# The way from the output projection to the up projection: second norm's gains moved into the weights, halves of the products interleaved with turns

## The chip, the cores and the metric

One Trainium2 chip, one core of it. TensorE (PE) multiplies, VectorE (DVE), ScalarE (ACT) and GpSimd (POOL) work on the results, and SyncE (SP) issues every DMA from one queue, in order. Each engine works through its own list of instructions in order and waits at the first one whose inputs or buffers are not ready. The metric is the time of one execution on the device, in microseconds (us): the median of three runs.

## The reference

One layer of an encoder: 1024 positions, 1024 channels, all in float32. What matters here is the step from the mixing sub-layer to the channel sub-layer.

```
y = concat(rmsnorm(ya, out_norm_a), rmsnorm(yb, out_norm_b)) @ w_o
x = x + rmsnorm(y, norm_mix_post)
h = rmsnorm(x, norm_ffn_pre)          # h = x / rms(x) * gain, gain has one value per channel
u = dwconv(h @ w_up, conv_w, conv_b)  # w_up: 1024 x 5632, width-3 convolution along the sequence
g, v = u[..., :2816], u[..., 2816:]
y = (gelu(g) * v) @ w_down
x = x + rmsnorm(y, norm_ffn_post)
```

## The kernel before

**Products.** Every float32 matrix is split into a high part that the multiplier takes exactly and a low part (ACT copies the high part, DVE or POOL subtracts it from the source), and a product is three matmuls: high by high, high by low, low by high. An instruction multiplies a 128x128 weight by 128x512 columns.

**The mixing sub-layer** ends with the output projection `o`, eight tiles of 128 positions (`t` = 0 to 7). Each tile takes 24 matmuls in two halves of 512 channels (`o_steps`, L1097); a half's accumulator is evacuated by DVE (L1107). Tiles 0 and 1 run under the last attention heads (events written at times of a plan); tiles 2 to 7 are written out by hand at L1301 to L1340. The rows that tile `t` needs are copied and split by `o_rows` (L1088): half of them are read from DRAM (`yd2`, L1090), the other half are in SBUF (`B["y"]`) once the last heads are normalised (`finish_steps`, L275).

**Two norms** follow for each tile (`o_norms`, L1111): ACT squares and sums the row, the root is taken, DVE or POOL multiplies by the gain of the first norm (L1117: on POOL for tiles 2 to 5), DVE scales and adds the residual (L1118), the sum is stored (L1119), ACT squares again, and DVE multiplies by root and by the second gain, `gffn` (L1123). That gain is read twice from DRAM as a 128x1024 broadcast.

**The up projection** works on 22 column tiles `f`. For each it has a tile `g` and a tile `v` of weights (loaded by `up_raw`, 512 KB each) and makes seven products (`up_product`, L1244), numbered 1 to 7, in place of the eight half-sized products of a 2x2 block scheme: weights are combined first (`up_prep`, L1225: DVE forms the sum `S`, ACT and POOL split it), the activations are combined too (`late_sums`, L1280), and the results are added afterwards (L1264 to L1274). A product is 12 matmuls. Each combination of the activations (5, 6, 7, 3, 4; 1 and 2 need none) is turned by TensorE: `late_turn` (L1290) does four 128x128 transposes into one of two PSUM banks `tr`, ACT copies the high part out, DVE the low part. The sums need both halves of the sequence, so tiles 4 to 7 decide.

**Order around the change.** The order of the calls is the priority; the framework then fixes each engine's list when the kernel is built, by its own estimate of when inputs are ready. `tc.issue_after(x)` holds a block's instructions behind instruction x on x's engine. After the hand-written o tiles, products (f, n) = (0,1), (0,2), (1,1), (1,2) run, each followed by the sums and four turns of one tile (L1352), then the turns for combination 4, then the remaining ten products of f = 0 and 1 in pairs (L1411), then f = 2 to 21, seven products each. Weights are prepared five products ahead (`AHEAD`). When the last product of an f is done, `conv_gate(f)` (L1372) does the convolution, the gelu and the gate with ACT and DVE.

**Buffers.** A new tile takes the memory of tiles freed before and waits for their last users. PSUM has eight banks of 128x512: two for `om` (o halves and small sums), two for `tr`, and four for `u`, the accumulators of even f, at this point. Copies `c1` of product 1 lie in a pool (`h2q`) that covers the memory of the o stage (`po`).

Of the kernel before, what the change touches and what calls it, by code (L numbers as in the profile page):

```python
# [37 lines left out]
def layer_kernel(  # L38
# [122 lines left out]
    gcols = cp.t([P, 16], "gcols")  # L161
# [256 lines left out]
    def small_columns():  # L418

        gr = pa.t([P, 512], "ph", bufs=PH)[:16, :P]  # L420
# [9 lines left out]
        nc.tensor.transpose(pt[:, 384:397], gr[:13, :], ident[:13, :13])  # L430
        nc.vector.tensor_copy(cvt.rearrange("p a b -> p (a b)"), pt[:, : 8 * NFF])
        nc.vector.tensor_copy(gcols[:, :13], pt[:, 384:397])
# [655 lines left out]
    def o_rows(q, yt, ys):  # L1088
        cs = slice(256 * q, 256 * q + 256)
        nc.sync.dma_start(yt, yd2[:, :, cs].rearrange("k p t -> p k t"))  # L1090
# [20 lines left out]
    def o_norms(t, junk, gpost, gffn, rsqrt=rsqrt_newton):  # L1111
# [11 lines left out]
        nc.vector.scalar_tensor_tensor(y, x2, rr, gffn, op0=ALU.mult, op1=ALU.mult)  # L1123
# [7 lines left out]

    def early_tiles():
        O["gpost"] = w4("wh")
        nc.sync.dma_start(O["gpost"], g_mix_post.partition_broadcast(P))
        O["gffn"] = w4("wh")
        nc.sync.dma_start(O["gffn"], g_ffn_pre.partition_broadcast(P))
# [9 lines left out]
    def early_norms(t):  # L1146
        o_norms(t, pa.t([P, S], "tmp", bufs=2), O["gpost"], O["gffn"])

    EARLY, EARLY_N = 2, 2
    NORM_V, NORM_P = [0, 1, 6, 7], [2, 3, 4, 5]  # L1150
# [38 lines left out]
    def late_rows(q):  # L1189
        ys = two_ys() if q == 2 else [xr.t([P, 2, 4, P], "x4", F32R), O["p"].t([P, 2, 4, P], "ys", F32R)]  # L1190
        o_rows(q, quarter_tile(po, QB), ys)
# [7 lines left out]
    def late_o(t):  # L1199
        for f in o_steps(t, om_bank):  # L1200
            f()

    def late_norms(t):
        o_norms(t, junk.pop() if junk else po.t([P, D], "jk"), gpost, gffn, rsqrt_cols)
# [3 lines left out]
    RAW, PREP, SUM = {}, {}, {}  # L1208

    def up_raw(f):  # L1210
        RAW[f] = []
        for w in range(2):
# [3 lines left out]
            RAW[f].append(wf)  # L1216

    count = []

    def w_tile():  # L1220

        count.append(0)
        return (pf if len(count) <= 4 or len(count) % 2 else pf2).t([P, 2, 4, P], "w", F32R, bufs=4)

    def up_prep(f, n):  # L1225
        if f not in RAW:
            up_raw(f)
# [4 lines left out]
        if n in terms:  # L1232
            src = SUM[f, n] = pf2.t([P, 4, P], "S", bufs=4)
# [8 lines left out]
    UP, MOV, CP = {}, {}, {}  # L1242

    def up_product(f, n):  # L1244
        if n == 1:
            if f % 2 == 0:
                UP[f] = [pu0.t([P, 2, 512], "u", bufs=2) for _ in range(2)]
# [10 lines left out]
        for k in range(4):  # L1258
            first, last = n in (1, 5, 2) and k == 0, k == 3
            mm(bank, w[:, 0, k], m[:, 0, k], start=first, stop=False, skip_group_check=True)  # L1260
            mm(bank, w[:, 0, k], m[:, 1, k], start=False, stop=False, skip_group_check=True)  # L1261
            mm(bank, w[:, 1, k], m[:, 0, k], start=False, stop=last, skip_group_check=True)  # L1262
        if n in (1, 5, 6):
            CP[f, n] = CP.pop("first", None) or (cpp if n == 1 else ap_).t([P, 512], f"c{n}", bufs=2)  # L1264
# [8 lines left out]
        if n == 3:  # L1273
            nc.vector.tensor_tensor(bank, bank, CP[f, 6], op=ALU.add)  # L1274

# [4 lines left out]
    def late_sums(t):  # L1280
# [4 lines left out]
        nc.vector.tensor_tensor(l[:, K0], h[:, K0], l[:, K0], **sub)  # L1285
        nc.gpsimd.tensor_tensor(h[:, K0], h[:, K1], h[:, K0], **sub)
        nc.vector.tensor_tensor(t2, h[:, K1], l[:, K0], **sub)
        nc.gpsimd.tensor_tensor(l[:, K1], l[:, K1], t2, **sub)
# [12 lines left out]
    gffn = bcast_row(po, g_ffn_pre, "gffn")  # L1301
# [3 lines left out]
    gpost = bcast_row(po, g_mix_post, "gpost")  # L1305
    fin = finish_steps(3, B, [], (2, 3), lambda: quarter_tile(po, QB), om_bank)
# [10 lines left out]
    fin[7]()  # L1317
    early_transpose(1)
    late_rows(2)
    late_norms(2)  # L1320
    group_rsqrt(1, slice(4, 8), rsqrt_cols)
    late_rows(3)
# [5 lines left out]
    late_o(4)  # L1328
    early_transpose(2)
    late_norms(4)  # L1330
    late_o(5)
    early_transpose(3)
    late_norms(5)
    up_raw(1)
    late_o(6)
    late_norms(6)
    late_o(7)
    for n in (1, 2):
        up_prep(1, n)
    late_norms(7)  # L1340
    po.free()
    O["p"].free()
    pwo.free()
    pu1 = {"v": Pool("pu1v", space=PSUM)}
    h2q = Pool("h2T1")
    MOV.update({1: B0[:, :, 0:4], 2: B0[:, :, 4:8]})
    MOV[4] = h2q.t([P, 2, 4, 512], "T4", F32R)
    cpp = h2q
    CP["first"] = h2q.t([P, 512], "c1", bufs=2)
    for n in (5, 6, 7, 3):  # L1350
        MOV[n] = h2q.t([P, 2, 4, 512], f"T{n}", F32R)
    for t, (f, n) in zip(range(4, 8), ((0, 1), (0, 2), (1, 1), (1, 2))):  # L1352
        up_product(f, n)
        late_sums(t)
        for n in (5, 6, 7, 3):
            late_turn(t, n)
    for t in range(4, 8):
        late_turn(t, 4)
# [52 lines left out]
    seq = [(f, n) for n in (5, 6, 7, 3, 4) for f in range(2)] + [(f, n) for f in range(2, NFF) for n in ORDER]  # L1411
# [238 lines left out]
```

## Time and profile before

| | |
|---|---|
| median of 3 runs | 1500.83 us (1500.44 to 1502.06) |
| profiled execution | 1505.44 us, its span 1503.4 us |
| PE busy | 1416.5 us, 94% of the span, 6481 matmuls |
| DVE, ACT, POOL busy | 972.3, 704.9, 533.2 us |
| mean granted clock of TensorE | 0.970 |

The span is the time from the first to the last instruction. A granted clock of 1.00 is TensorE at 2.4 GHz, 0.50 is 1.2 GHz. Attention ends at about 778 us of the span, the o tiles and norms lie between 756 and 846 us, and from 905 us on the up projection runs its regular pattern to about 1300 us.

### The profile page before, as it was taken

Reading aid. Unit: us, or ns where it says so; the run is one execution under the profiler, and the core shown is the slowest. Engines: PE = TensorE matmul, PEld = TensorE weight load, DVE = VectorE, ACT = ScalarE, POOL = GpSimd, SP = SyncE. Lnnn points to the kernel's source line nnn. Section 1 sums busy time; section 2 is a strip of 40 time slices with the busy share of each in tenths; the row PEclk is TensorE's granted clock in tenths of the full one; section 3 lists DMA queues with packets and bytes.
Section 4 is the critical chain, followed back from the end, with each engine's and each line's share of the span. In section 5 each row is a group of like instructions: output and inputs, shape, how many; then the busy total and the mean of one; then the engine's idle time right before and its main releaser. Section 6 shows DMA issues by size and latency. Waiting matters only on the chain.

```text
span 1503.4 us, 18725 instructions
## 1 busy us (share of the span) xinstructions
PE 1416.5 (94%) x6481; PEld 1120.9 (75%) x6481; DVE 972.3 (65%) x1637; ACT 704.9 (47%) x1274; POOL 533.2 (35%) x443
## 2 busy tenths in 40 slices
PE   7999999997899999889998689999999999999998
PEld 6788887876676676556666567888888888788886
DVE  6465453438976766532487768766677765884687
ACT  5244343325455556534645354444444444554444
POOL 3133222216444544322425355555555553000110
PEclk9999999997999999989999899999999999999999
DMA  5522343555433212521116123333333321964435
GB/s 188 118 72 67 76 101 87 169 134 187 99 70 104 63 36 69 145 75 29 57 56 205 48 70 112 106 106 105 105 105 106 106 91 58 336 219 144 126 98 196
DMA packets 135903, 167.06 MB, mean 111 GB/s; under 512 B 17443, under 2 KB 93616, under 8 KB 134144
## 3 DMA queue, kind: packets, MB, share of 16 engines
q1 hardware_dynamic: 135808, 165.87, 37.2%
q8 instruction: 51, 0.84, 0.2%
q14 instruction: 44, 0.36, 0.1%
HBM read 106.12 MB, written 39.43 MB: 97 GB/s over the span
## 4 chain that ended last, share of the span: by engine, by line
PE 52%; DVE 5%; POOL 4%; ACT 3%; issue 3%; DMA 2%; SPq 0%; DVEq 0%; POOLq 0%; ACTq 0%
PE u_pu L1260 4%; PE u_pu L1262 4%; PE u_pu L1261 4%; PE v_pu1v L1260 3%; PE v_pu1v L1262 3%; PE v_pu1v L1261 3%; PE X_acc L1501 2%; PE X_acc L1502 2%; PE X_acc L1500 2%; PE Y_acc L1501 2%; PE Y_acc L1500 2%; PE Y_acc L1502 2%; PE g_pu1g L1260 2%; PE g_pu1g L1262 2%; PE g_pu1g L1261 2%
## 5 line engine op out<-in xcount | busy, mean ns | idle before, releaser
L348 POOL TENSOR_TENSOR pl_pA<-sx_pA,ph_pA 128x512 fp32r<-128x512 f32 (+1 forms) x125 | 162.8, 1307 | 266.3 <-ACT sx_pA L92 122.7
L1240 POOL TENSOR_TENSOR w_pF<-S_pF,w_pF 128x512 fp32r<-128x512 f32 x88 | 129.4, 1472 | 106.3 <-ACT w_pF L92 77.0
L1240 POOL TENSOR_TENSOR w_pF<-wf_pF,w_pF 128x512 fp32r<-128x512 f32 x66 | 88.9, 1349 | 96.7 <-ACT w_pF L92 96.6
L95 PE MATMUL proj_psx<-hT_hT,wh_pA 128*128 128x512 f32 (+2 forms) x304 | 120.6, 397 | 0.0
L96 PE MATMUL proj_psx<-hT_hT,wh_pA 128*128 128x512 f32 (+2 forms) x304 | 119.0, 391 | 0.1
L97 PE MATMUL proj_psx<-hT_hT,wl_pA 128*128 128x512 f32 (+2 forms) x304 | 118.9, 391 | 0.0
L945 DVE TENSOR_REDUCE m_pA<-mx_psy 128x1 f32<-128x512 f32 x126 | 83.9, 685 | 38.9 <-PE mx_psy L944 38.3
L92 ACT ACTIVATE w_pF<-ar_pD 128x512 fp32r<-128x512 f32 x77 | 48.5, 630 | 99.6 <-PE Y_acc L1502 44.0
L92 ACT ACTIVATE w_pF<-S_pF 128x512 fp32r<-128x512 f32 x88 | 55.3, 628 | 80.2 <-PE u_pu L1262 41.2
L92 ACT ACTIVATE sx_pA<-s_ps 128x512 f32<-128x512 f32 x128 | 75.0, 597 | 27.9 <-PE s_ps L970 13.2
L1260 PE MATMUL u_pu<-T_h2T,w_pF 128*128 128x512 f32 x220 | 85.7, 390 | 1.5 <-ACT c_h2T L92 1.5
L1262 PE MATMUL u_pu<-T_h2T,w_pF 128*128 128x512 f32 x220 | 85.7, 390 | 0.6 <-POOL w_pF L1240 0.6
L1261 PE MATMUL u_pu<-T_h2T,w_pF 128*128 128x512 f32 x220 | 85.8, 390 | 0.0
L1462 DVE TENSOR_TENSOR w_pF<-ar_pD,w_pF 128x512 fp32r<-128x512 f32 x77 | 55.5, 721 | 46.3 <-ACT w_pF L92 46.3
L337 DVE TENSOR_TENSOR sx_pA<-s_ps,tab_pA 128x256 f32<-128x256 f32 (+1 forms) x128 | 48.3, 410 | 53.4 <-PE s_ps L607 34.1
L537 DVE CUSTOM_DVE_ANT_0 mx_psx<-mx_psx,tab_pA 128x256 f32<-128x256 f32 (+1 forms) x112 | 47.1, 420 | 48.9 <-PE mx_psx L534 45.6
L229 POOL TENSOR_TENSOR wl_pA<-wf_pA,wh_pA 128x256 fp32r<-128x256 f32 x48 | 36.9, 794 | 115.0 <-ACT wh_pA L92 102.3
L348 DVE TENSOR_TENSOR pl_pA<-sx_pA,ph_pA 128x512 fp32r<-128x512 f32 (+1 forms) x67 | 48.7, 730 | 35.9 <-ACT sx_pA L92 34.2
L1501 PE MATMUL X_acc<-w_pF,w_pF 128*128 128x512 f32 x176 | 68.9, 391 | 2.4 <-DVE w_pF L1464 2.4
L92 ACT ACTIVATE ph_pA<-s_ps 128x512 fp32r<-128x512 f32 x85 | 50.4, 596 | 38.6 <-PE s_ps L970 38.2
L1500 PE MATMUL X_acc<-w_pF,w_pF 128*128 128x512 f32 x176 | 68.5, 389 | 0.0
L1502 PE MATMUL X_acc<-w_pF,w_pF 128*128 128x512 f32 x176 | 68.5, 389 | 0.0
(451 smaller groups left out, 4143.8 us busy)
## 6 DMA issues: line engine op xcount, KB each, us to landing
wf_pF<-in_w_up SPq DMA_DIRECT2D x44, 512.0 KB
ar_pD<-aD_dr SPq DMA_DIRECT2D x77, 256.0 KB
head_pA<-x_xr SPq DMA_DIRECT2D x22, 512.0 KB
aD_dr<-vt_aT SPq DMA_DIRECT2D x44, 256.0 KB
B_pD<-in_w_down SPq DMA_DIRECT2D x44, 256.0 KB
aD_dr<-gt_aT SPq DMA_DIRECT2D x33, 256.0 KB
wf_pA<-in_w_in SPq DMA_DIRECT2D x16, 512.0 KB
head_pA<-x_xr SPq DMA_DIRECT2D x24, 256.0 KB
```

What stands on the lines that cost most here:

```text
L92: nc.scalar.activation(o, i, func, **kw)
L95: i = mm(ps, ah, bh, start=first, stop=False)
L96: mm(ps, ah, bl, start=False, stop=False)
L97: mm(ps, al, bh, start=False, stop=last)
L348: e.tensor_tensor(pl[:, cs], pf[:, cs], f32(ph[:, cs]), op=ALU.subtract)
L1240: nc.gpsimd.tensor_tensor(w[:, 1], src, f32(w[:, 0]), op=ALU.subtract)
L1260: mm(bank, w[:, 0, k], m[:, 0, k], start=first, stop=False, skip_group_check=True)
L1261: mm(bank, w[:, 0, k], m[:, 1, k], start=False, stop=False, skip_group_check=True)
L1262: mm(bank, w[:, 1, k], m[:, 0, k], start=False, stop=last, skip_group_check=True)
L1500: mm(bank, wa[:, 0, ts], wb[:, 0], start=first, stop=False, skip_group_check=True)
L1501: mm(bank, wa[:, 0, ts], wb[:, 1], start=False, stop=False, skip_group_check=True)
L1502: mm(bank, wa[:, 1, ts], wb[:, 0], start=False, stop=last, skip_group_check=True)
```

## The change

The second norm's gain is no longer multiplied into the rows. It is read once as columns (`gcols` 13 to 20, in `small_columns`), and ACT multiplies it into the raw weights, one 128x128 block at a time and in place (`up_scale`): 16 blocks for each f, all of f = 0 and of f = 1 at once, and for later f four blocks at each of four of the preparations of the f before. The load of the next f is written one f earlier. In `o_norms` the last step becomes an ACT scaling by the root, and all first-gain products go to DVE. Both broadcasts of `gffn` are gone.

The rows of the last two quarters are loaded into tiles of their own early on (`late_rows_load`). The o tiles of even t use two `u` banks in place of `om`. The first four products follow the last o tile at once, ahead of the norms of tiles 6 and 7. The copies `c1` move to the pool `h2p`, the first `S`, `c5` and `c6` tiles to memory that is free earlier. The turns of combination 5 come behind product (1,2); each of the turns for 6, 7, 3 and 4 is cut in two pairs, one ahead of and one inside the product of f = 0 before it. The POOL half of the sums is a function of its own behind them (`late_sums2`). The five products of f = 0 run first, `conv_gate(0)` follows them, then the five of f = 1.

```diff
@@ small_columns
-        for r0, src in ((0, g_q), (3, g_kv), (5, g_a), (9, g_b)):
+        for r0, src in ((0, g_q), (3, g_kv), (5, g_a), (9, g_b), (13, g_ffn_pre)):
...
@@ o_norms
-        nc.vector.scalar_tensor_tensor(y, x2, rr, gffn, op0=ALU.mult, op1=ALU.mult)
+        act(y, x2, scale=rr)
...
+    def late_rows_load(q):
+        cs = slice(256 * q, 256 * q + 256)
+        YQ[q] = (O["p"] if q == 2 else po).t([P, 512], "yq").rearrange("p (k t) -> p k t", k=2)
+        nc.sync.dma_start(YQ[q], yd2[:, :, cs].rearrange("k p t -> p k t"))
...
-    NORM_V, NORM_P = [0, 1, 6, 7], [2, 3, 4, 5]
+    NORM_V = range(NT)
...
     def late_o(t):
-        for f in o_steps(t, om_bank):
+        bank = om_bank
+        if t % 2 == 0:
+            u = pu0.t([P, 2, 512], "u", bufs=2)
+            halves = [u[:, 0, :], u[:, 1, :]]
+            bank = lambda: halves.pop(0)
+        for f in o_steps(t, bank):
             f()
...
+    def up_scale(n):
+        for wf, k in SCALE[:n]:
+            act(wf[:, k], wf[:, k], scale=gcols[:, 13 + k : 14 + k])
+        del SCALE[:n]
...
     def up_prep(f, n):
-        if f not in RAW:
-            up_raw(f)
+        if 0 < f < NFF - 1 and f + 1 not in RAW and (f, n) != (1, 1) and (f, n) != (1, 2):
+            up_raw(f + 1)
+        elif n not in (1, 5):
+            up_scale(4)
...
         for k in range(4):
+            if k == 2 and mid:
+                mid()
...
-            CP[f, n] = CP.pop("first", None) or (cpp if n == 1 else ap_).t([P, 512], f"c{n}", bufs=2)
+            CP[f, n] = C0.pop() if f == 0 and n > 1 else (h2p if n == 1 else ap_).t([P, 512], f"c{n}", bufs=2)
...
+    late_rows(2)
+    group_rsqrt(1, slice(4, 8), rsqrt_cols)
+    late_norms(2)
+    late_rows(3)
     early_transpose(1)
...
+    up_scale(16)
     for n in (1, 2):
         up_prep(0, n)
...
+    for f in range(2):
+        for n in (1, 2):
+            early = up_product(f, n)
+    late_norms(6)
     late_norms(7)
...
-    for t, (f, n) in zip(range(4, 8), ((0, 1), (0, 2), (1, 1), (1, 2))):
-        up_product(f, n)
-        late_sums(t)
-        for n in (5, 6, 7, 3):
+    for t in range(4, 8):
+        summed = late_sums(t)
+    def turn_two(n, t):
+        if n:
             late_turn(t, n)
+            late_turn(t + 1, n)
+    with tc.issue_after(early.ins):
+        turn_two(5, 4)
+        turn_two(5, 6)
     for t in range(4, 8):
-        late_turn(t, 4)
+        late_sums2(t)
+    for n, after in zip((5, 6, 7, 3, 4), (6, 7, 3, 4, None)):
+        with tc.issue_after(summed.ins):
+            up_prep(0, n)
+        turn_two(after, 4)
+        up_product(0, n, lambda: turn_two(after, 6))
...
-    seq = [(f, n) for n in (5, 6, 7, 3, 4) for f in range(2)] + [(f, n) for f in range(2, NFF) for n in ORDER]
+    conv_gate(0)
+    seq = [(1, n) for n in (5, 6, 7, 3, 4)] + [(f, n) for f in range(2, NFF) for n in ORDER]
```

## Rows read from the trace of the kernel before

**Rows 1.** Windows: us, then busy us (x instructions) per engine, PE clock, DMA

```profile
785.00:845.00 60.00, 46.76 (x215) 37.34 (x213) 50.25 (x70) 29.97 (x64) 31.23 (x18) 0.93 0.48 158
838.00:854.00 16.00, 7.41 (x27) 5.42 (x26) 12.17 (x13) 5.17 (x10) 7.11 (x5) 0.68 0.08 33
...
785.20:905.40 120.20, 95.64 (x430) 74.59 (x429) 91.46 (x120) 61.05 (x112) 57.22 (x37) 0.91 0.32 101
...
1000.00:1190.40 190.40, 190.40 (x841) 157.66 (x841) 132.97 (x141) 90.75 (x131) 99.16 (x70) 1.00 0.32 104
```

**Rows 2.** Timeline of PE: start, duration, instruction, [idle before it, releaser]

```profile
798.25 0.50 PE L95 MATMUL om_pwo<-w_wo,qr_qr 128*128 128x512 f32 x1 [2.99 <-ACT qr_qr L92]
...
800.69 0.80 PE L97 MATMUL om_pwo<-w_wo,qr_qr 128*128 128x512 f32 x1 [1.48 <-DVE qr_qr L1059]
801.29 0.63 PE L95 MATMUL om_pwo<-w_wo,qr_qr 128*128 128x512 f32 x1
801.71 0.63 PE L96 MATMUL om_pwo<-w_wo,qr_qr 128*128 128x512 f32 x1
...
822.53 0.47 PE L95 MATMUL om_pwo<-w_wo,ys_wo 128*128 128x512 f32 x1 [1.39 <-DVE x_xr L1107]
...
844.99 0.80 PE L1260 MATMUL v_pu1v<-h2T_h2T,w_pF 128*128 128x512 f32 x1 [6.36 <-ACT c_h2T L92]
...
880.19 0.50 PE L1260 MATMUL v_pu1v<-T_h2T,w_pF 128*128 128x512 f32 x1 [2.12 <-DVE g_pu1g L1270]
...
905.37 0.50 PE L1260 MATMUL u_pu<-T_h2T,w_pF 128*128 128x512 f32 x1 [1.50 <-ACT c_h2T L92]
```

**Rows 3.** Timeline of SP: loads of the second gain and of the rows

```profile
780.71 0.37 SPq L206 DMA_DIRECT2D gffn_pO<-in_norm_ffn_pre  x1
...
794.05 1.65 SPq L1090 DMA_DIRECT2D tmp_pO<-yd_dr  x2
```

**Rows 4.** Timeline of ACT between 790 and 845 us

```profile
797.78 0.72 ACT L92 ACTIVATE qr_qr<-tmp_pO 128x256 fp32r<-128x256 f32 x2 [1.49 <-DMA tmp_pO<-yd_dr]
...
842.90 0.58 ACT L92 ACTIVATE c_h2T<-u_pu 128x512 f32<-128x512 f32 x1
```

**Rows 5.** Groups on ACT: count | busy us, mean ns | idle before, releaser

```profile
L92 ACT ACTIVATE w_wo<-wf_pA,gcols_const 128x1024 fp32r<-128x1024 f32 x8 | 9.2, 1149 | 14.7 <-DMA wf_pA<-in_w_o 14.7
...
L92 ACT ACTIVATE ckv_lat<-x_xr 128x1024 fp32r<-128x1024 f32 x2 | 2.0, 1041 | 0.0
...
L92 ACT ACTIVATE wf_pA<-wf_pA 128x128 f32<-128x128 f32 x2 | 0.5, 303 | 1.7 <-DMA wf_pA<-in_w_in 1.7
```

**Rows 6.** Groups on DVE and POOL, the same columns

```profile
L1235 DVE TENSOR_TENSOR S_pF<-S_pF,wf_pF 128x512 f32<-128x512 f32 x22 | 27.3, 1239 | 10.2 <-POOL w_pF L1240 10.0
...
L1123 DVE SCALAR_TENSOR_TENSOR x_xr<-xt_pO,r_const,gffn_pO 128x1024 f32<-128x1024 f32 x4 | 8.1, 2030 | 0.1
...
L1117 DVE TENSOR_TENSOR PA_woA<-PA_woA,wh_pA 128x1024 f32<-128x1024 f32 x2 | 2.4, 1217 | 0.0
...
L1117 POOL TENSOR_TENSOR x_xr<-x_xr,gpost_pO 128x1024 f32<-128x1024 f32 x2 | 6.1, 3046 | 6.8 <-ACT jk_pO L92 6.8
```

**Rows 7.** Chain that ended last, around one pair of turns: start us, us, what

```profile
857.06 0.67 PE tr_pwt L1295 x4
...
857.75 0.60 ACT T_h2T L92
...
858.38 0.70 DVE T_h2T L1299
```

**Rows 8.** The same chain at product (1,5) of the up projection

```profile
878.92 0.49 ACT c_aT L92
...
879.43 0.71 DVE g_pu1g L1270
```

**Rows 9.** Timeline of ACT in the regular part of the up projection

```profile
1025.89 0.62 ACT L92 ACTIVATE w_pF<-wf_pF 128x512 fp32r<-128x512 f32 x1
...
1028.18 0.63 ACT L92 ACTIVATE w_pF<-S_pF 128x512 fp32r<-128x512 f32 x1 [1.66 <-PE u_pu L1262]
```

More of the change, by code (lines that the diff above doesn't have):

```diff
@@ L160, in layer_kernel @@
     nc.vector.memset(ones, 1.0)
-    gcols = cp.t([P, 16], "gcols")
+    gcols = cp.t([P, 24], "gcols")
     ssq = cp.t([P, 4, NT], "ssq")
@@ L1086, in o_load, with o_rows @@
         nc.sync.dma_start(xt, x[t * P : (t + 1) * P, :])
-    def o_rows(q, yt, ys):
+    def o_rows(q, yt, ys, loaded=False):
         cs = slice(256 * q, 256 * q + 256)
-        nc.sync.dma_start(yt, yd2[:, :, cs].rearrange("k p t -> p k t"))
+        if not loaded:
+            nc.sync.dma_start(yt, yd2[:, :, cs].rearrange("k p t -> p k t"))
         for j in range(2):
@@ L1216, in up_raw @@
             RAW[f].append(wf)
+            SCALE.extend((wf, k) for k in range(KT))
+    def up_scale(n):
+        for wf, k in SCALE[:n]:
+            act(wf[:, k], wf[:, k], scale=gcols[:, 13 + k : 14 + k])
+        del SCALE[:n]
     count = []
@@ L1240, in up_prep, with up_product @@
         nc.gpsimd.tensor_tensor(w[:, 1], src, f32(w[:, 0]), op=ALU.subtract)
-    UP, MOV, CP = {}, {}, {}
-    def up_product(f, n):
+    UP, MOV, CP, SUM0, C0 = {}, {}, {}, [], []
+    def up_product(f, n, mid=None):
         if n == 1:
             if f % 2 == 0:
-                UP[f] = [pu0.t([P, 2, 512], "u", bufs=2) for _ in range(2)]
+                UP[f] = [pu0.t([P, 2, 512], "u", bufs=2) for _ in range(2)][::-1]
             else:
@@ L1261, in up_product @@
             mm(bank, w[:, 0, k], m[:, 1, k], start=False, stop=False, skip_group_check=True)
-            mm(bank, w[:, 1, k], m[:, 0, k], start=False, stop=last, skip_group_check=True)
+            done = mm(bank, w[:, 1, k], m[:, 0, k], start=False, stop=last, skip_group_check=True)
         if n in (1, 5, 6):
-            CP[f, n] = CP.pop("first", None) or (cpp if n == 1 else ap_).t([P, 512], f"c{n}", bufs=2)
+            CP[f, n] = C0.pop() if f == 0 and n > 1 else (h2p if n == 1 else ap_).t([P, 512], f"c{n}", bufs=2)
             act(CP[f, n], bank)
@@ L1274, in up_product @@
             nc.vector.tensor_tensor(bank, bank, CP[f, 6], op=ALU.add)
+        return done
     def early_transpose(t):
@@ L1285, in late_sums, with late_sums2 @@
         nc.vector.tensor_tensor(l[:, K0], h[:, K0], l[:, K0], **sub)
+        return nc.vector.tensor_tensor(t2, h[:, K1], l[:, K0], **sub)
+    def late_sums2(t):
+        h, l = rows(t), rows(t - 4)
+        K0, K1 = HALF
+        sub = dict(op=ALU.subtract)
         nc.gpsimd.tensor_tensor(h[:, K0], h[:, K1], h[:, K0], **sub)
-        nc.vector.tensor_tensor(t2, h[:, K1], l[:, K0], **sub)
-        nc.gpsimd.tensor_tensor(l[:, K1], l[:, K1], t2, **sub)
+        nc.gpsimd.tensor_tensor(l[:, K1], l[:, K1], B["sum", t], **sub)
     def late_turn(t, n):
@@ L1339, in layer_kernel @@
         up_prep(1, n)
+    pwo.free()
+    pu1 = {"v": Pool("pu1v", space=PSUM)}
+    MOV.update({1: B0[:, :, 0:4], 2: B0[:, :, 4:8]})
+    for f in range(2):
+        for n in (1, 2):
+            early = up_product(f, n)
+    late_norms(6)
     late_norms(7)
```

50 lines of the change are left out of this document (22 added, 28 removed).

## Prediction

> **What bounds the kernel now.** I read the windows first, then TensorE's (PE's) own timeline, then the chain of waits and the groups by duration. From 905 us of the span on PE never pauses: 841 matmuls in 190.40 us, 0.226 us each, at clock 1.00 [rows 1]. There a change gains nothing, it can only lose. The passage from 785.2 to 905.4 us is another matter: PE is busy 95.64 of 120.20 us, so 24.6 us are idle, and the mean clock of 0.91 says that part of the busy time ran at 1.2 GHz [rows 1]. The reader should see in PE's timeline what each pause waits for [rows 2]: the copied rows of o tile 4 (2.99 and 1.48 us), an `om` bank (twice, the longer time 1.39 us), a copy c1 that stands on ScalarE (ACT) behind the last norm (6.36 us), the sum for f = 1 (2.12 us), and f = 2 behind two gates at once (1.50 us). After the pauses of 2.99 and 1.48 us the matmuls come 0.42 us apart instead of 0.226 (801.29 to 801.71) [rows 2]; in the stretch with the longest pause PE is busy 7.41 of 16 us at a clock of 0.68 [rows 1]. So the passage is a chain of waits and not PE work, and its end is the first matmul of product (2,5) at 905.37 [rows 2]. I rebuild the time of that matmul.
>
> **The change part by part.**
>
> *Rows loaded early.* The two loads stood on SyncE at 794.05 [rows 3], ACT waited for them until 797.78 [rows 4], PE until 798.25. With the loads done long before, PE goes on at 798.25 - 2.99 = 795.3. The second gain's 512 KB broadcast at 780.71 [rows 3] and the one in the attention tail go, two 256 KB loads move ahead on the same queue: cost nothing, since SyncE then only waits less.
>
> *Even o tiles in `u` banks.* The waits for `om` go. What is late next is nothing on PE: the rows are there. O tiles 4 to 7 are 96 matmuls, 21.7 us; the four turn groups of tiles 2 and 3 between them take about 0.5 us each, an estimate under the 0.67 of four transposes [rows 7], since neighbours overlap. Products (0,1), (0,2), (1,1), (1,2) are 48 matmuls, 10.9 us, and (1,2) waits for a copy of (1,1), which shares its tile, 0.8 us with the handing over (0.58 in rows 4). PE is through at 795.3 + 21.7 + 2.0 + 10.9 + 0.8 = 830.7.
>
> *Norms.* VectorE (DVE) loses the product with the second gain, 2.03 us each when GpSimd (POOL) runs beside it, and takes four products with the first gain at 1.22 instead of 3.05 on POOL [rows 6]. It is relieved. ACT pays. It was busy 29.97 us between 785 and 845 [rows 1]. Added are seven row scalings of 1.15 us (an ACT instruction that takes its factor from a column: 1149 ns against 1041 without [rows 5]), 8.0 us, and the 32 weight scalings of f = 0 and 1. One is at least the 0.25 us at which two without a column came (0.5 us busy for two of 303 ns), and at most 303 + 108 = 0.41 us alone [rows 5]; I take 0.30, the first plus half the surcharge, since they come in runs. That is 9.6 us, with bounds of 8.0 and 13.1. ACT then has 47.6 us of work from 785 and could end at 832.6 if it never waited. It waits for half of that stretch now; I give it 3.4 us of waiting, so 836, bounds 832.6 and 846. Two sums of 0.7 us on DVE and one turn (0.67 + 0.60 + 0.70 [rows 7]) follow: combination 5 is complete at 839.4. The turns of tiles 4 to 6 run before that, in PE's pause from 830.7. The copies c1 no longer wait for the o stage's memory, so the 6.36 us go, but 8.7 us between 830.7 and 839.4, with only turns in them, take their place.
>
> *Turns between halves of products.* Before, two turns took 0.67 + 0.60 + 0.70 and the handing over between the three, 2.15 us, with PE waiting for ACT and DVE [rows 7]. Now four turns stand beside each of four products. A product is 2.7 us on PE, with four turns 4.7; the way through ACT and DVE is 4.3; DVE has four copies of 0.70, a sum `S` of up to 1.24 [rows 6] and one result of 0.7, 4.7. Lower bound 4.7, upper 7.0 if nothing overlaps; I take 5.0, near the lower one, because the product gives PE work while the banks are emptied. Four steps and a fifth product: 839.4 + 20.0 + 2.7 = 862.1.
>
> *Five products of f = 1 without f = 0 between them.* This part costs. (1,6) must wait for the copy of (1,5) and the sum after it, 0.49 + 0.71 us and the handing over [rows 8], 1.6 us as I count; (1,7) for the copy of (1,6), 0.9; and the first weight tile lies on memory that the last result of f = 0 frees, 0.5. With 13.6 us of products that is 878.7; product (2,1) takes 2.7, so (2,5) is due at 881.4. The gate of f = 0 now runs beside f = 1, so the 1.50 us at 905.37 go. For two pauses after which the matmuls come at half clock I add 1.6 us each (eight matmuls, 0.2 us more for each, as at 801.29): 884.6.
>
> *Up projection.* Each f puts 16 scalings on ACT, 4.8 us at 0.30, beside 90.75 / 10 = 9.1 us [rows 1] of the 19.04 that 84 matmuls take. They stand in fours (1.2 us) ahead of a preparation, and ACT is idle 1.66 us before such a preparation [rows 9], so I put them at nothing. Without that cover they would cost up to what the rival below says. The loads come one f earlier in the program, but only when the same buffers are free. The eight more gain columns in the small load at the start cost nothing.
>
> Sum: 905.4 - 884.6 = 20.8 us less. Made against the profiled execution (1505.44 us, 4.6 above the median) that gives 1484.6; taken off the median of 1500.83 it is **1480 us**.
>
> **The rivals.**
>
> *The norms still end late.* Each tile's chain goes ACT, DVE, ACT, DVE, ACT, and ACT works in order: it may stand still before a square while a scaling behind it could run. If the last scaling comes at the upper bound of 846, all after it shifts by 10: 1490. For it speaks that ACT is the fullest engine there; against it, that POOL's 3.05 us leave each chain.
>
> *Little friction.* ACT ends at 832.6 (3.4 less), the steps take 4.7 (1.2 less), the 3.0 us of f = 1 and the 3.2 us of half clock are covered: 10.8 us less, 1469. Against it stands that f = 1 has nothing between its products.
>
> *The scalings gate the products (slower).* ACT must copy product 1 before 6 may write and 6 before 7. If the four scalings stand ahead of these two copies and the idle time is elsewhere, each f loses up to 2.4 us, 48 us over the 20 that follow: 1528. It decides from 20.8 / 20 = 1.04 us per f. Against it: with them ACT has 13.9 of 19.04 us, and between product 1 and 6 a product of 2.7 us lies. The Trainium skill, "ScalarE: Activation LUTs", section "Rules for kernel authors", speaks for this rival: it gives multiplications to VectorE and not to ScalarE. By that rule the change moves the gain to the wrong engine; this trace has DVE busier than ACT both in the passage (50.25 against 29.97) and in the regular part (132.97 against 90.75) [rows 1], so here I side with the row.
>
> *It doesn't do what it says.* The lists are fixed when the kernel is built, by estimates; the turns may end up ahead of the products, or a wait for a late tile stand before work that was ready. Steps of 7.0 instead of 5.0 cost 8.0, late norms 10, and two more microseconds leave 1500.
>
> **How the numbers follow.** Forecast (1474 to 1486) 0.50, late norms 0.22, little friction 0.13, gating 0.08, no effect 0.07. Faster is the first three, 0.85, less a little for late norms with longer steps: 0.84. Same (0.2%, 3 us, about what runs of this kernel can tell apart) 0.06; slower 0.10, the gating and a part of the last. The range of 1469 to 1496 takes in little friction and most of the late norms and leaves out gating and no effect.
>
> **What would show it.** In the changed kernel's profile: PE without a pause from 795 to about 830; ACT busy over 90% there; the first product with combination 5 at 839 and steps of 5.0 with four turns each; pauses of 1 to 2 us before (1,6) and (1,7); the first matmul of (2,5) near 885; and 84 matmuls in 19.04 us from there on. Wrong if ACT's last scaling is past 842, if a step takes over 6, or if PE shows pauses in the regular part.

## The result, and the profile after

The change made the kernel slower: 1524.06 us median of 4 runs (1523.12 to 1525.71) against 1500.63 us beside it, a ratio of 1.0155, 95% interval 1.014 to 1.0171. Forecast was 1480 us.

I split the difference of the two profiled spans (1523.9 - 1503.4 = 20.5 us) at marks that both traces have. The medians differ by 23.4 us: the profiled execution of the kernel before took 1505.44 us, 4.8 more than the median beside it, that of the changed kernel 1525.71, 1.7 more. Some 3 us between two traces can thus be the spread of executions. "Pauses" and "rate" are counted over all matmuls of a stretch, from start to start: 0.2267 us for each is the bare time, what a gap of over 0.30 has beyond that is a pause, and what is left is the rate.

| stretch | before | after | difference |
|---|---|---|---|
| up to the attention's last score matmul | 771.3 | 766.9 | -4.4 |
| from there to the first matmul of (2,5), the passage | 134.1 | 126.9 | -7.2 |
| from there to the first matmul of the down projection | 378.2 | 404.0 | +25.8: pauses 0.1 to 20.1, rate 0.0 to 5.8 |
| from there to the last matmul | 212.9 | 219.3 | +6.4: pauses 3.4 to 4.0, rate 0.2 to 6.1 |

(The last 6.8 us after it differ by 0.2.) So the passage got shorter, and two things that I had put at nothing cost over four times what it brought: pauses in the up projection, and matmuls that come slower.

Windows of the changed kernel (us, busy us and instructions of PE, PEld, DVE, ACT, POOL, PE clock, DMA share, GB/s; PEld is PE loading weights):

```profile
785.00:845.00 60.00, 47.05 (x224) 38.80 (x223) 44.69 (x66) 45.48 (x103) 25.05 (x17) 0.89 0.39 130
830.00:845.00 15.00, 4.59 (x18) 3.89 (x19) 11.56 (x17) 7.36 (x15) 10.06 (x6) 0.55 0.09 36
1000.00:1190.40 190.40, 182.97 (x785) 146.36 (x784) 127.18 (x128) 125.04 (x273) 91.38 (x67) 1.00 0.29 93
1350.00:1450.00 100.00, 100.00 (x431) 80.48 (x430) 54.01 (x81) 47.57 (x88) 6.42 (x4) 1.00 0.41 125
```

In the regular part there are 785 matmuls where the kernel before has 841 [rows 1], and PE is idle for 7.4 us of it. The last window lies in the down projection, which the change doesn't touch: PE is busy throughout, at full clock, and yet does 431 matmuls. The same stretch of work in the kernel before:

```profile
1335.00:1435.00 100.00, 100.00 (x443) 82.81 (x442) 58.22 (x88) 48.58 (x90) 6.40 (x4) 1.00 0.43 134
```

A busy PE is thus not a PE at the same rate; only the count shows it.

PE's timeline in the passage of the changed kernel, to be held against [rows 2]:

```profile
824.36 0.50 PE L1285 MATMUL v_pu1v<-h2T_h2T,w_pF 128*128 128x512 f32 x1 [0.69 <-ACT c_h2T L92]
838.86 1.97 PE L1326 MATMUL tr_pwt<-ident_const,PA_woA 128*128 128x128 f32 x8 [10.61 <-DVE T_h2T L1330]
842.37 0.80 PE L1285 MATMUL u_pu<-T_h2T,w_pF 128*128 128x512 f32 x1 [1.54 <-ACT T_h2T L92]
...
860.70 1.43 PE L1326 MATMUL tr_pwt<-ident_const,PA_woA 128*128 128x128 f32 x8 [1.31 <-DVE T_h2T L1330]
869.70 0.50 PE L1287 MATMUL g_pu1g<-T_h2T,w_pF 128*128 128x512 f32 x1 [0.47 <-POOL w_pF L1263]
874.91 0.50 PE L1285 MATMUL u_pu<-h2T_h2T,w_pF 128*128 128x512 f32 x1 [2.60 <-ACT w_pF L92]
878.37 0.80 PE L1287 MATMUL u_pu<-h2T_h2T,w_pF 128*128 128x512 f32 x1 [2.72 <-POOL w_pF L1263]
```

The pauses for rows, `om` banks and the copy c1 are gone. In their place stand one of 10.61 us before the turned products and two at (2,1). Half clock stands behind the first and the last: matmuls come 0.43 us apart from 845.17 and from 878.96 on. ACT in the same stretch; the squares (`jk`) belong to the norms of tiles 6 and 7:

```profile
826.56 1.06 ACT L92 ACTIVATE jk_pO<-xt_pO 128x1024 f32<-128x1024 f32 x1 [2.25 <-DVE xt_pO L1120]
...
827.94 1.04 ACT L92 ACTIVATE jk_pO<-x_xr 128x1024 f32<-128x1024 f32 x1
...
833.90 1.06 ACT L92 ACTIVATE jk_pO<-xt_pO 128x1024 f32<-128x1024 f32 x1 [3.60 <-DVE xt_pO L1120]
...
835.61 1.15 ACT L92 ACTIVATE x_xr<-xt_pO,r_const 128x1024 f32<-128x1024 f32 x1 [0.23 <-DVE r_const L181]
```

Now the regular part. First the waits of PE and of ACT in the up projection (total us, times, longest), then the instructions around one of them:

```profile
PE v_pu1v L1285 <- ACT c_h2T L92: 7.2, 9, 1.2
PE u_pu L1285 <- ACT c_h2T L92: 7.2, 8, 1.2
...
ACT wf_pF L92 <- DMA wf_pF<-in_w_up: 85.8, 32, 3.7
```

```profile
1004.13 1.35 POOL L1263 TENSOR_TENSOR w_pF<-wf_pF,w_pF 128x512 fp32r<-128x512 f32 x1 [0.35 <-ACT w_pF L92]
...
1005.51 9.19 SPq L1229 DMA_DIRECT2D wf_pF<-in_w_up  x2
...
1009.37 0.70 ACT L92 ACTIVATE wf_pF<-wf_pF,gcols_const 128x128 f32<-128x128 f32 x2 [3.43 <-DMA wf_pF<-in_w_up]
...
1018.08 0.40 ACT L92 ACTIVATE wf_pF<-wf_pF,gcols_const 128x128 f32<-128x128 f32 x1 [1.92 <-DMA wf_pF<-in_w_up]
1018.38 1.04 ACT L92 ACTIVATE gt_aT<-gt_aT 128x1024 f32<-128x1024 f32 x1
1019.34 0.57 ACT L92 ACTIVATE c_h2T<-u_pu 128x512 f32<-128x512 f32 x1
```

This is to be read as a circle. POOL's split of a preparation is the last reader of an old weight tile; as it ends (1005.48), SP sends off the load into that tile (1005.51); ACT has a scaling of that load next in its list and stands until 1009.37, although the weights are wanted one f later; the preparations queued behind it then free the tile of the second load, and ACT stands again until 1018.08. Only then come gelu and the copy of product 1, and PE, which needs that copy for product 6, starts it at 1019.96 after 0.87 us idle. Each f from 3 to 19 has one such pause (0.40 to 1.24 us); f = 2 has one that waits for a DVE sum, and f = 20 and 21, behind the last scaling at 1248 us, have none. All 352 scalings took 114.7 us busy, 394 ns each, 0.30 in a run.

### The profile page after: what moved, and what is told of

Its sections match the earlier page's. It is cut to its first block, busy times and chain, and to the rows that moved or that the text cites. A ratio compares the mean times of both kernels' runs of the same rounds, so it can differ in the third digit from the quotient of the medians.

```text
span 1523.9 us, 19072 instructions
## 1 busy us (share of the span) xinstructions
PE 1427.1 (94%) x6481; PEld 1117.2 (73%) x6481; DVE 968.6 (64%) x1633; ACT 809.1 (53%) x1634; POOL 517.7 (34%) x439
## 4 chain that ended last, share of the span: by engine, by line
PE 31%; ACT 14%; DMA 9%; DVE 6%; POOL 4%; issue 4%; SPq 0%; POOLq 0%; DVEq 0%; ACTq 0%
DMA wf_pF<-in_w_up 7%; ACT wf_pF L92 5%; POOL w_pF L1263 3%; PE X_acc L1550 2%; ACT w_pF L92 2%; PE X_acc L1551 2%; PE X_acc L1549 2%; PE Y_acc L1549 2%; PE Y_acc L1550 2%; PE Y_acc L1551 2%; ACT gt_aT L92 2%; PE proj_psy L97 2%; PE proj_psy L95 1%; PE proj_psy L96 1%; PE mx_psy L944 1%
## 5 line engine op out<-in xcount | busy, mean ns | idle before, releaser
L1263 POOL TENSOR_TENSOR w_pF<-S_pF,w_pF 128x512 fp32r<-128x512 f32 x84 | 119.3, 1421 | 153.1 <-ACT w_pF L92 144.9
L92 ACT ACTIVATE wf_pF<-wf_pF,gcols_const 128x128 f32<-128x128 f32 x352 | 114.7, 394 | 92.9 <-DMA wf_pF<-in_w_up 89.9
L1285 PE MATMUL u_pu<-T_h2T,w_pF 128*128 128x512 f32 x220 | 88.5, 402 | 9.6 <-ACT c_h2T L92 7.2
L92 ACT ACTIVATE sx_pA<-s_ps 128x512 f32<-128x512 f32 x128 | 75.1, 597 | 27.1 <-PE s_ps L970 12.5
L1286 PE MATMUL u_pu<-T_h2T,w_pF 128*128 128x512 f32 x220 | 87.0, 395 | 0.0
L1287 PE MATMUL u_pu<-T_h2T,w_pF 128*128 128x512 f32 x220 | 86.8, 394 | 0.0
L1550 PE MATMUL X_acc<-w_pF,w_pF 128*128 128x512 f32 x176 | 70.3, 400 | 1.9 <-DVE w_pF L1513 1.7
L1549 PE MATMUL X_acc<-w_pF,w_pF 128*128 128x512 f32 x176 | 70.3, 400 | 0.0
L1551 PE MATMUL X_acc<-w_pF,w_pF 128*128 128x512 f32 x176 | 70.3, 399 | 0.0
```

The lines of the kernel that those rows point to most:

```text
L92: nc.scalar.activation(o, i, func, **kw)
L1263: nc.gpsimd.tensor_tensor(w[:, 1], src, f32(w[:, 0]), op=ALU.subtract)
L1287: done = mm(bank, w[:, 1, k], m[:, 0, k], start=False, stop=last, skip_group_check=True)
L1549: mm(bank, wa[:, 0, ts], wb[:, 0], start=first, stop=False, skip_group_check=True)
L1550: mm(bank, wa[:, 0, ts], wb[:, 1], start=False, stop=False, skip_group_check=True)
L1551: mm(bank, wa[:, 1, ts], wb[:, 0], start=False, stop=last, skip_group_check=True)
```

## The experiments

The time beside the kernel before is given as a ratio with its 95% interval; each batch had its own runs of the kernel before, medians 1500.6 to 1502.9 us. Pauses and rate are those of the up projection from (2,5) on, where no other stretch is named.

### Where the slower matmuls come from

The gain table grew from 64 to 96 bytes per row and lies below all tiles of its side of the memory. By the allocator's addresses, which no trace shows, all that lies left moved from 992 bytes past a multiple of 1024 to a multiple: half of the weight tiles, and the activations that TensorE multiplies them with. The right weight tiles stayed at 992. `w_tile` takes its tiles from both sides in turn (left for odd numbers in the order of the preparations), and slow products alternate with it: by that count they are those with a right weight tile, the ones that did not move.

```diff
-    gcols = cp.t([P, 24], "gcols")
+    gcols = cp.t([P, 32], "gcols")
```

> The changed kernel with a table of gain columns of 128 bytes per row instead of 96, nothing else; every tile behind it on the left side of the memory moves by 32 bytes, so the weight tiles lie 32 bytes past a multiple of 64 instead of on one. Placement theory: the matmuls that come 0.2333 us apart are back at 0.2267 in the up and the down projection, 12 us less, about 1512 us. Rival (the 352 scalings and the work around them disturb the matmuls wherever the tiles lie): nothing changes, 1524 us. The pauses of 20.0 us between the matmuls of the up projection stay by both.

1523.87 us, 1.0136 (1.0114 to 1.0158). Up projection: rate 5.8 to 2.6 (products with a right weight tile 0.229 instead of 0.233 us for a matmul), but pauses 20.1 to 27.1. Down projection, where each product takes one operand from either side: rate 6.1, unchanged. Neither theory as put.

The kernel before with `gcols = cp.t([P, 24], "gcols")`:

> The kernel before with the gain table of 96 bytes per row, nothing else. Placement theory: half the products of the up projection and all of the down projection come 0.2333 us apart, 12 us more, about 1512 us. Rival (scalings disturb the matmuls): no scalings here, so nothing changes, 1500.6 us.

1514.87 us, 1.0087 (1.0069 to 1.0104): 13 us for 32 bytes and nothing else. PE's timeline, first a product with a right weight tile, then one with a left:

```profile
1006.11 0.40 PE L1260 MATMUL v_pu1v<-T_h2T,w_pF 128*128 128x512 f32 x1
1006.35 0.39 PE L1261 MATMUL v_pu1v<-T_h2T,w_pF 128*128 128x512 f32 x1
1006.58 0.40 PE L1262 MATMUL v_pu1v<-T_h2T,w_pF 128*128 128x512 f32 x1
1006.81 0.39 PE L1260 MATMUL v_pu1v<-T_h2T,w_pF 128*128 128x512 f32 x1
...
1008.88 0.39 PE L1260 MATMUL g_pu1g<-h2T_h2T,w_pF 128*128 128x512 f32 x1
1009.11 0.39 PE L1261 MATMUL g_pu1g<-h2T_h2T,w_pF 128*128 128x512 f32 x1
1009.34 0.39 PE L1262 MATMUL g_pu1g<-h2T_h2T,w_pF 128*128 128x512 f32 x1
1009.56 0.39 PE L1260 MATMUL g_pu1g<-h2T_h2T,w_pF 128*128 128x512 f32 x1
```

Three matmuls take 0.70 us in the first product and 0.68 in the second. Durations hardly tell; starts do. Rate lost: 5.6 us in the up projection, 6.0 in the down projection, the same as in the changed kernel. The left tile is fast although it moved; the right one is slow although it stayed. Placement, without scalings, is shown to cost this.

Two other places, one run each. The changed kernel with `pf.t([P, 16], "pad")` at the bottom of the pool (64 past a multiple of 1024):

> The changed kernel with an unused tile of 64 bytes per row at the bottom of the pool that holds the weight tiles. They move from a multiple of 1024 to 64 past one. If every multiple of 64 is slow: matmuls stay at 0.2333 us, 1524 us. If only multiples of a larger power of two are: 0.2267 us, about 1512 us.

1523.78 us; rate 8.5 up, 7.0 down, slow on both sides (0.230 us with a left weight tile, 0.2335 with a right one). And the kernel before with 32 bytes of padding ahead of the left weight tiles and 992 behind, so that the activations behind them move by a whole 1024:

> The kernel before with 32 bytes of padding ahead of the weight tiles and 992 behind them: left weight tiles on a multiple of 1024, everything behind them (moving operands too) 992 past one as before. If the weight tile's place decides: every other product of the up projection at 0.2333 us, +5.5 us. If weight and moving operand both have to lie on the multiple: all at 0.2267 us, no change (1501 us).

1512.15 us; rate 5.9 up, in every other product as the first answer has it, and 6.1 down, which it did not have. But the slow half is now the other one: with a left weight tile a matmul takes 0.2329 us, with a right one 0.2270, where the run with 24 columns has 0.2266 and 0.2332. Here a left tile first, then a right one:

```profile
1004.15 0.40 PE L1262 MATMUL g_pu1g<-h2T_h2T,w_pF 128*128 128x512 f32 x1
...
1004.85 0.40 PE L1262 MATMUL g_pu1g<-h2T_h2T,w_pF 128*128 128x512 f32 x1
...
1006.25 0.39 PE L1262 MATMUL v_pu1v<-T_h2T,w_pF 128*128 128x512 f32 x1
...
1006.93 0.39 PE L1262 MATMUL v_pu1v<-T_h2T,w_pF 128*128 128x512 f32 x1
```

So it is not the place of the weight tile by itself. In both runs the slow products are those whose two operands were shifted against each other, and those whose operands kept their distance modulo 1024 are fast or nearly so; the down projection, with one operand from either side, is slow in every run that shifted the left side alone. The run with 64 bytes of padding doesn't fit wholly: there left weight tiles and activations moved alike and still took 0.230 us. What in the two addresses decides stays open.

The remedy puts `eps` and `ones` into one tile, so that all lies as before:

```diff
-    eps = cp.t([P, 1], "eps")
+    eo = cp.t([P, 3], "eo")
+    eps, ones = eo[:, 0:1], eo[:, 1:3]
-    ones = cp.t([P, 2], "ones")
```

> The changed kernel with the first of these edits alone: the tiles lie where they lay before, scalings as in the change. Placement theory: 1524 - 12 = 1512 us, all matmuls at 0.2267 us, pauses of 20 us as before the edit. If part of the slower matmuls comes from the scalings' reads and writes: more than 1515 us.

1520.68 us, 1.0122 (1.0101 to 1.0143). Windows:

```profile
1000.00:1190.40 190.40, 179.05 (x778) 144.91 (x777) 126.26 (x128) 125.88 (x275) 87.68 (x65) 1.00 0.29 93
1350.00:1450.00 100.00, 100.00 (x443) 82.78 (x442) 58.23 (x88) 48.33 (x90) 6.40 (x4) 1.00 0.43 136
```

The down projection is back at 443. In the up projection the rate is back too (0.7 us lost), but the stretch takes 405.0 us as before: the pauses grew to 26.2 by what the matmuls gained. So PE doesn't set the time of an f there; the circle through ACT and the loads does.

### What makes the pauses

The scalings of f = 2 to 21 left out, with the 128-byte table:

```diff
-            SCALE.extend((wf, k) for k in range(KT))
+            SCALE.extend((wf, k) for k in range(KT if f < 2 else 0))
```

> The changed kernel with the 128-byte table and without the weight scalings of f = 2 to 21 (the gain of the second norm is left out there); loads, order of preparations and everything else stay. Theory that the scalings gate the products: the pauses of 20.0 us in the up projection go, each f takes 19.04 us, and with placement mended too 1524 - 20 - 12 = 1492 us. Rival (the earlier loads or the new order of preparations make the pauses): the pauses stay and the time is that of the run with the 128-byte table alone.

1499.48 us, 0.9989 (0.9975 to 1.0004); pauses 2.4, all before 914 us. The window shows 837 matmuls and ACT at the 90.7 us of [rows 1]:

```profile
1000.00:1190.40 190.40, 190.40 (x837) 156.96 (x836) 127.96 (x140) 90.71 (x130) 101.39 (x70) 1.00 0.32 104
```

The scalings, not the loads or the new order, make the pauses. Next, with the tiles put back, the value half's eight put behind the copy of product 1, after `up_product` in the loop:

```diff
+        if n == 1:
+            with tc.issue_after(CP["copy"].ins):
+                up_scale(8)
```

> The changed kernel with two edits: two small constants share a tile, so that all weight tiles lie where they lay before; and the eight scalings of the value half of a load are put behind ScalarE's copy of product 1 of the next-but-one step, so that ScalarE stands on the load only after that copy. Theory (ScalarE's wait for the load in front of that copy makes the pauses): pauses of 20.0 us fall under 3, matmuls at 0.2267 us, 1524 - 12 - 18 = 1494 us or less. Rival (ScalarE simply has too much to do with the scalings): the pauses stay near 20 us at other places, about 1512 us.

1540.61 us, 1.0252 (1.0231 to 1.0273); pauses 43.5. The wait that I had moved was not the only one: ACT now stood on the gate half's load, 4.4 and 6.9 us in two f (95.2 us in 17 waits over the stretch), and the gate's steps, gelu and the copy of product 1 came late behind it. With the scalings on DVE:

```diff
-            act(wf[:, k], wf[:, k], scale=gcols[:, 13 + k : 14 + k])
+            nc.vector.tensor_scalar(wf[:, k], wf[:, k], gcols[:, 13 + k : 14 + k], None, op0=ALU.mult)
```

> The previous kernel (tiles placed as before) with the 352 scalings on VectorE instead of ScalarE, at the same places of the program. If the engine's order behind a load is what costs: VectorE stands on the load in front of the sums that the next product waits for, and pauses of 10 to 25 us stay, 1503 to 1517 us. If it is ScalarE's load (multiplications belong on VectorE): the pauses go, about 1492 us.

1535.03 us, 1.0214 (1.0186 to 1.0242); pauses 40.2. DVE hardly waited for loads (group line: count, busy us, mean ns, idle before), but it was busy 180.7 of 190.4 us, and the sums that products wait for came late:

```profile
L1236 DVE TENSOR_SCALAR wf_pF<-wf_pF,gcols_const 128x128 f32<-128x128 f32 x352 | 135.7, 439 | 2.4 <-DMA wf_pF<-in_w_up 1.9 <-POOL w_pF L1263 0.5
```

So here the amount of work is the likely cause, which I had not expected; that is read from the busy time, and no run with another order on DVE was made. The Trainium skill ("ScalarE: Activation LUTs", "Rules for kernel authors") gives multiplications to VectorE, with a figure for bf16; these scalings are in float32, and the pair of runs with the scalings on ACT and on DVE speaks against it in this kernel (1520.68 against 1535.03 us, 394 ns each on ACT against 439 on DVE). Both halves late, and none in the preparations from f = 2 on:

```diff
+        if f > 1 and n in (1, 5):
+            with tc.issue_after(CP["copy"].ins):
+                up_scale(8)
```

> The changed kernel, tiles placed as before, all 352 scalings kept on ScalarE, but both halves of a load put late: the eight of the gate half behind the copy of product 1, the eight of the value half behind the copy of product 5, one f after their load. Theory (ScalarE, in order, stands in front of a load that has just been sent off, and the preparations behind it free the buffers of the next load, so that two loads of 3.7 us stand in the chain of each f): no waits of ScalarE for a load are left, the pauses of 26 us fall under 4, the up projection takes 382 us instead of 405, 1521 - 23 = 1498 us. Rival (16 scalings are too much for ScalarE in 19.04 us): pauses of over 15 us stay, 1512 us or more.

1562.24 us, 1.0391 (1.0368 to 1.0414); pauses 66.8, the theory's number missed by the widest margin. ACT no longer waited for loads. But the scalings came just before the preparations, so DVE's four sums `S` (0.7 us the first, 1.6 to 1.8 us the others, with POOL at work beside them) bunched in front of the sum of product 2, and PE waited for that one, here in the odd f (15.6 us more in the even ones):

```profile
PE g_pu1g L1285 <- DVE g_pu1g L1295: 20.5, 9, 2.5
```

Early scalings stand on the load; late ones hand their lateness on. To separate waiting from work, the scalings were turned to a scratch tile:

```diff
+                act(SCR[0], ident, scale=gcols[:, 13 + k : 14 + k])
```

> The changed kernel, tiles placed as before, with the 320 scalings of f = 2 to 21 turned to a scratch tile: same engine, same number, same size, same places in the program, but they wait for no load and nobody waits for them (the gain is left out in these f). Theory (waits and their order make the pauses): the pauses of 26 us fall to 3, 1521 - 23 = 1498 us. Rival (the work itself, 16 scalings per f, is too much for ScalarE): pauses stay over 15 us, 1510 us or more.

1502.17 us, 1.0001 (0.9989 to 1.0013); pauses 8.3. With nothing to wait for, ACT ran them ahead, so they bunched: 28 per f instead of 16 in the window below, none after 1100 us. In this window ACT was nearly full:

```profile
960.00:1080.00 120.00, 116.81 (x506) 93.92 (x505) 89.19 (x84) 114.46 (x253) 54.72 (x43) 1.00 0.31 99
```

Even so PE lost only 3.2 us there, 0.5 per f, and all pauses lie before 1094 us. The amount is the smaller part. Last, an order set by hand: four scalings after the gate's second step, the copy of product 1, eight, gelu, the copy of product 5, four; with the passage edits below.

```diff
+            with tc.issue_after(last.ins):   # the gate's second step
+                up_scale(4)
...
+            with tc.issue_after(CP["copy"].ins):
+                up_scale(8 if n == 1 else 4)
+                if n == 1:
+                    GATE.pop()()             # gelu and what follows
```

> Scalings kept on ScalarE, tiles placed as before, the passage edits added, and ScalarE's order per f set by hand: four scalings behind the gate's second step, the copy of product 1, eight scalings of the value half, gelu, the copy of product 5, four scalings; each load is on its way for over 5 us by then. Theory (with an order in which ScalarE never stands on a load and no copy that gates a product stands behind scalings, they cost nothing): pauses under 5 us, 1487 us or less. Rival (no place in 19.04 us is free of somebody who waits): pauses over 15 us, 1500 us or more.

1494.02 us, 0.9948 (0.9933 to 0.9963). Pauses 3.1, none of them ACT standing on a load; all 352 scalings are there. In the last two runs of the next section, alike but for the scalings and the gain in the rows, the pauses are 4.2 us with scalings and 3.7 without. That settles it: in the up projection the scalings cost nothing but by their place in ACT's list. The median misses the 1487 of the theory, since the passage kept the wait of the next section.

### What the passage is worth

The passage alone, with the gain multiplied into the rows as before, no scalings, the old table:

> The passage of the changed kernel alone: early rows, o tiles in other banks, new order of norms, turns between halves of products, f = 1 alone, loads one f earlier; but the second gain is multiplied into the rows as before (VectorE, beside the factor of the norm), no weight scalings, and the gain table and so the tiles lie where they lay before. Theory (the passage brings 11.6 us, scalings and placement cost all that is lost): 1501 - 11.6 = 1489 us, a little less if ScalarE, freed of 32 scalings of 0.39 us in the passage, ends earlier. Rival (the passage is earlier only because VectorE lost the product with the gain): six products of 2.03 us come back on VectorE, 12 us, about 1500 us.

1498.74 us, 0.9976 (0.9963 to 0.999). From the attention's last score matmul (767.4) to (2,5) it takes 125.8 us, the changed kernel 126.9: DVE's product with the gain did not bring the time back. The 11.6 us of my expectation were 905.4 - 893.8 and counted the earlier end of the attention in; that end lay between 763.5 and 771.2 in the runs with the new passage and between 769.0 and 771.3 in three with the old, so how much of it is the passage's (the means are 766.6 and 770.1) is not shown. Against 132.2 to 135.9 in the kernel before and its two runs with moved tiles, the passage brings 5 to 10 us in the traces, less 2.4 of pauses that come later. The medians give less: 3.2 us for the whole kernel (1.5 to 5.6 by the interval), since the profiled execution of the kernel before lay 4.6 us above its median and that of this kernel 2.4 us under its own.

Two edits on that kernel: (2,1) held behind (1,4) on PE, and the norms of tiles 6 and 7 written step by step for both (both squares, then both products with the gain, and so on).

```diff
+            if (f, n) == (2, 1):
+                es.enter_context(tc.issue_after(added.ins))
             added = up_product(f, n)
```

> The kernel with the gain in the rows (the passage alone), with product (2,1) held behind (1,4) on TensorE, as the program has them; in the run of the passage alone it stood ahead of (1,6) and waited 2.6 us for ScalarE and 2.7 us for GpSimd, with half clock behind. Theory (an order fixed by estimates puts a product with late weights ahead of ready ones): 5 us of waits and 2 us of half clock go, about 1492 us. Rival (the weights of f = 1 are late all the same, GpSimd prepares them one after the other at 1.7 us each): the waits stand before (1,6) and (1,7), 1498 us.

1494.09 us, 0.9948 (0.9929 to 0.9967), nearer to the theory's 1492 than to 1498, but not by the passage, which by the trace is as long as before (126.3 us against 125.8). The pauses at (2,1) and the later 2.5 us went, and a wait for a DVE sum took their place:

```profile
876.34 0.79 PE L1286 MATMUL v_pu1v<-T_h2T,w_pF 128*128 128x512 f32 x1 [5.56 <-DVE g_pu1g L1296]
```

> The kernel with the gain in the rows, with the norms of tiles 6 and 7 written step by step for both instead of one after the other. In the changed kernel the square of tile 7 started at 827.94 us, behind the second square of tile 6, though its rows were complete at 817.8. Theory (the last two norms stand one behind the other in the engines' order): the pause of 10.6 us of TensorE before the products with turned sums falls to 4 to 6, about 1493 us. Rival (VectorE is full there and the two norms only share it): no change, 1498 us.

1496.69 us, 0.9956 (0.9942 to 0.997). The pause before the turned products, 10.61 us in the changed kernel and 11.55 in the run of the passage alone, is 7.95, with 1.07 ahead of it: 2.5 us, half of what I expected. But the products ahead of the pause ended later, and from the attention's last score matmul to the first turned product it is 76.4 us, against 76.6 in the run of the passage alone. So by the traces the edit brought 0.2 us here and 1.8 beside the other edit (75.3 us against 77.1), and the intervals of this run and of the passage alone overlap. In the run of both edits DVE is busy 15.00 of the 15 us from 830, which speaks for the rival. Both together:

> The two edits of the passage together. If each is worth what its theory says and they do not touch the same wait: 1498 - 6 - 5 = 1487 us. If the earlier norms only lead into a longer wait for the weights of f = 1: 1492 us.

1491.54 us, 0.9926 (0.9907 to 0.9945), near the second case. The wait of 5.54 us at (1,6) stayed. First try at it, the gate of f = 0 later on DVE:

> The kernel of both passage edits, with the gate of f = 0 put behind the sum of product (1,5) on VectorE; there VectorE did the gate's four steps and its last product, which waits for ScalarE's function table and gelu, before that sum, and TensorE waited 5.5 us. Theory (order on VectorE): the 5.5 us and 2 us of half clock behind them go, 1491.5 - 7 = 1485 us. Rival (the gate must end before product (2,5) can write its bank, so the wait moves there): 1490 us.

1493.38 us, 0.994 (0.9924 to 0.9955): no gain, wait 4.88. With the gate out of the way, eight weight sums stand ahead of that sum on DVE, four of them of f = 2. Putting those of f = 2 behind it, with scalings by hand and with the gain in the rows:

```diff
+                if seq[ready][0] == 2 and SUM15:
+                    es.enter_context(tc.issue_after(SUM15[0]))
                 up_prep(*seq[ready])
```

> The kernel with scalings ordered by hand and all passage edits, with the weight sums of f = 2 put behind VectorE's sum of product (1,5): there they stood ahead of it, 865.8 to 872.5 us, and TensorE waited 4.9 us until 873.25. Theory (VectorE's order): the 4.9 us and about 2 us of half clock behind them go, 1494 - 6 = 1488 us. Rival (the gate of f = 0 or GpSimd's splits are due next): 1492 us or more.

1488.69 us, 0.9919 (0.9905 to 0.9932), the fastest. PE's timeline, and the window of the regular part:

```profile
834.63 1.12 PE L1327 MATMUL tr_pwt<-ident_const,PA_woA 128*128 128x128 f32 x4 [6.87 <-DVE T_h2T L1331]
...
866.20 0.50 PE L1288 MATMUL g_pu1g<-T_h2T,w_pF 128*128 128x512 f32 x1 [1.02 <-POOL w_pF L1264]
870.18 0.50 PE L1286 MATMUL v_pu1v<-T_h2T,w_pF 128*128 128x512 f32 x1 [1.42 <-DVE g_pu1g L1296]
```

```profile
1000.00:1190.40 190.40, 190.23 (x836) 156.32 (x835) 134.92 (x140) 133.83 (x290) 98.49 (x70) 1.00 0.32 104
```

ACT has 133.83 us of work here, 8.8 more than in the changed kernel, and PE is idle for 0.17.

> The same edit on the kernel with the gain in the rows and all passage edits (no scalings). Theory: 1493 - 6 = 1487 us; rival: 1491 us or more. Against the kernel with scalings by hand it shows which way of applying the gain is cheaper once nothing waits: by the passage alone (VectorE's product with the gain, 2.0 us for each of six tiles, against 32 scalings on ScalarE) the scalings should be 2 to 4 us ahead.

1489.31 us, 0.9927 (0.9914 to 0.9941): the same as with scalings, within the intervals. The 2 to 4 us that I gave the scalings are not seen in the medians. In the two traces the passage is 3.7 us shorter with scalings (117.6 us against 121.3); an attention that ended 1.4 us later, 0.8 us in the up and 1.4 us in the down projection took it back.

## Why the prediction was wrong

*The step that failed* is the up projection: "They stand in fours (1.2 us) ahead of a preparation, and ACT is idle 1.66 us before such a preparation [rows 9], so I put them at nothing." The size was right (0.30 us each in a run), and so was the idle time. I asked whether ACT has room and not what each scaling waits for. I had even written that the loads come "only when the same buffers are free", but not that ACT would stand on them in order. Cost: 20 us of pauses.

*The rival "the scalings gate the products"* had the right engine and the right copy, and a break-even of 1.04 us per f; I gave it 0.08. Its price was work in front of a copy, up to 2.4 us; what happened was a wait, some 1.0 us per f, 25.8 us over the stretch together with the rate.

*"The eight more gain columns ... cost nothing"* failed as well: 12 us of slower matmuls by the run of the kernel before with 24 columns. No row of before could show it. In the changed kernel it cost the down projection 6 us; the 6 of the up projection were hidden under the circle, as the run with the tiles put back shows.

*The passage.* Its first half came as written: PE is through its products at 827.2 (forecast 830.7, with an attention that ended 4.4 earlier), ACT 94% busy from 785 to 815 (but 84% from 795 to 830, where the prediction named over 90), and the last scaling of rows ends at 836.76 (836). That number was right for a partly wrong reason: ACT was not full to the end but stood 2.25 and 3.60 us on DVE, because the norm of tile 7 started behind that of tile 6 (square at 827.94). The first turned product was due at 839.4 and came at 842.37, behind two DVE sums, two turns and a weight sum of 1.79 us, in order. Steps took (868.60 - 842.37 - 2.7) / 4 = 5.9 us on average, not 5.0: from first matmul to first matmul the first step took 8.3 (842.37 to 850.71, at half clock up to 848), the third 6.4 with a wait of 1.31. The five products of f = 1 took 25.2 us with (2,1), forecast 22.5; the waits at (1,6) and (1,7) did not come, two others did. So (2,5) is at 893.8 instead of 884.6. Of the 11.6 us that it came earlier, 4.4 lie ahead of the passage.

*What would show it.* Of the three signs named, the last scaling past 842 did not occur; a step over 6 did, in two of the four, and so did the third, pauses in the regular part.

## What to carry to other kernels

An engine that works in order must not have next in its list an instruction that waits for a load just sent off, whatever room it has: ask of each added instruction what it waits for, what is queued behind it, and whether that frees the buffer of the next load. Moving one such wait only uncovers the next; the order that worked was written for a whole period at once. And when a constant grows, compare the count of matmuls per window in a stage that the change doesn't touch.

## What the runs showed of the hardware

- Matmuls of the same shape, with PE busy throughout at full clock, came 0.2267 us apart or up to 0.2343, and it followed from where the tiles lie: 32 bytes cost 13 us. Fast in both projections were only the runs with all tiles 992 bytes past a multiple of 1024. With a shift of 32 bytes the slow products were those whose weight tile and activations had moved against each other, whichever of the two had moved (0.2332 against 0.2266 us in the kernel before with 24 columns, 0.2329 against 0.2270 with the padding of 32 and 992); with both 64 bytes past a multiple it was 0.230. The Trainium skill ("TensorE: Matmul & The Clock Gate", "Step-by-step: what each phase is for") says that loading the next weights takes no read bandwidth from the running product; no run here shows whether the loading or something else makes the difference. Why is open.
- A 128x128 scaling by a column took 394 ns on ACT (0.30 us each in a run of several) and 439 on DVE, mean of 352 each.
